# One step of a two-layer attention and RWKV-7 trunk: the mixer's state kept with keys as rows, and the samples' gate computed in the variance's bank

## The chip, the cores and the metric

The kernel runs as one launch on one core of a Trainium2 chip. The metric is device time in microseconds (us), the median of several runs. Five engines work side by side, each on its own queue of instructions: TensorE (PE in the profile; its weight loads have a row of their own, PEld), VectorE (DVE), ScalarE (ACT), GpSimd (POOL) and SyncE (SP), which here only issues DMAs.

## The reference

Two layers, 1024 prompt positions and 8 sample positions, width 1024, all in fp32. Each layer projects its input, runs windowed attention on one half of the columns and an RWKV-7 mixer with 8 heads of 64 on the other, projects both back, and adds a feed-forward part of width 4096. The change is in the mixer:

```
def step(S, inp):                                   # S: [value, key] for each head
    r_t, w_t, k_t, v_t, a_t, b_t = inp
    sa = einsum('bhvk,bhk->bhv', S, a_t)
    S = S * w_t[:, :, None, :] + sa[..., None] * b_t[:, :, None, :] + v_t[..., None] * k_t[:, :, None, :]
    return S, einsum('bhvk,bhk->bhv', S, r_t)
S_T, y = lax.scan(step, wkv0, xs)
mu = y.mean(-1); var = square(y - mu).mean(-1)      # per head
y = (y - mu) * rsqrt(var + GN_EPS) * gn_g + gn_b
y = (y + bonus) * g                                 # g = sigmoid(g_lo) @ gate_up
```

## The kernel before

**Work.** The prompt is cut into two halves of 512 positions; the 8 samples ride with the second. For each layer and half, the dense stream (`dense_stream`, `half`, `in_proj`) does the projections and the feed-forward part as matmuls in fp32r, three for each product (lines 389 to 391: high times high, low times high, high times low), with 256 to 512 moving columns. Beside it run the attention (`att_stream`), the mixer and the samples' attention (`kv_stream`).

**The mixer.** A unit is 256 positions of one pair of heads; there are 2 layers x 2 halves x 4 pairs x 2 = 32 units, each cut into four chunks of 64 positions (`cc` = 0 to 3, `tb, c = divmod(cc, 2)`). The first head of the pair lies on partitions 0 to 63, the second on 64 to 127. `stage1` prepares a unit, `stage2` carries the state through it, and `normed` does the GroupNorm and the gate. In `stage2`, after the inversion of the chunks' triangular matrices (lines 1308 to 1356), come two parts:

- The **pO part** (lines 1358 to 1376): for c = 0 and 1, a bank `o3` takes Pt times LB in its columns 0 to 127 and TV times LB in columns 128 to 255 (line 1370: lhsT is TV, 64 wide, and the contraction runs over all 128 partitions). One half of those 64 + 64 columns is the chunk's own share of the output y, the other its share of the new state. VectorE makes FG from columns 0 to 127.
- The **carry steps** (lines 1378 to 1395), one for each `cc`: the state Z, with keys as rows, is the stationary operand of line 1384, which adds to both halves of `o3`. The half that is the state then has values as rows and keys as columns. VectorE copies it to `St` (line 1386), TensorE transposes it with a product by the identity into the bank `pz` (line 1391), and VectorE scales it by the decay into the next Z (line 1393). The very first unit of a prompt starts without a state, so its first step has no product with Z.

**The gate.** `normed` sums y by a product with a block matrix (line 1417) and computes the gate for the 256 positions (line 1418) in one bank `pgm`, then the sum of squares (line 1431) in a bank `pgv`. In the last unit of a pair in the second half (8 units) a third bank, `pgd`, takes the gate of the 8 samples (line 1423); this stands ahead of the copy of the prompt's gate out of `pgm` (line 1426). All three have the tag "o", of which there are two banks; `o3` and line 1308's `pBV` use it as well. The tag "r" has one bank.

**The order on TensorE** is written at build time by the class `Streams` (lines 147 to 260): each stream is a generator that yields (planned cost, bank tag held and for how long, delay before its next piece, bank tag wanted). The planner always takes the first stream in the order s2 (stage2), norm, s1, att, post, kv that is ready, and otherwise the dense stream; delays are multiplied by 1.2 in the first phase and 2.2 later (`SLK`), and a turn away from the dense stream costs 280 planned ns. One turn can hold pieces of several streams. At run time TensorE executes that order strictly; the other engines' orders are made by the build's own scheduler.

Line 1004 is a gate of the dense stream: late in the first half's feed-forward part of the last layer it waits until the second half's mixer, attention and sample parts are all planned. In the attention, line 1623 delays a tile's transposition by 2500 + 4 x 640 planned ns for the widest tile, and line 1640 its output product.

Of the trace's names: `dps` are the dense banks, `pS`, `pET`, `pFT`, `po`, `pof` the attention's banks, `E` its scores, `pdo` those of `kv_stream`. A matmul in plain fp32 leaves two records in the trace (x4 is two matmuls); one in fp32r leaves one. "64*64" is the array tile that is used (rows * columns), "64x128" the output's partitions or rows and its columns.

Of the kernel before, what the change touches and what calls it, by code (L numbers as in the profile page):

```python
# [10 lines left out]
F32 = mybir.dt.float32  # L11
# [3 lines left out]
ALU = mybir.AluOpType  # L15
# [6 lines left out]
NB = 8  # L22
# [13 lines left out]
UN = 256  # L36
NU = HB // UN
# [229 lines left out]
def body(ctx, tc, I, O):  # L267
# [17 lines left out]
    def bank(tag, name):  # L285
        return ps.tile([128, 512], F32, tag=tag, bufs=BANKS[tag], name=name)
# [5 lines left out]
    def C(name):  # L292
        a, n = CAT[name]
        return cst[:, a:a + n]

    ident = C("ident")
    istk = C("istk")
# [805 lines left out]
    dd = {}  # L1103
# [207 lines left out]
    def stage2(l, h, p, u, s, st, Z, Zp):  # L1311

        AR, Wd, LB, TV, X, XT, bv, _ = st

        def other(c):
            return slice(64 * (1 - c), 64 * (1 - c) + 64)

        def halfof(t, c):
            return t.rearrange("p (b c) h s x -> p c h b s x", c=2)[64 * c:64 * c + 64, c]

        for lv in range(2):
            pb = bank("r", "pT1")
            q = small(pb, 0, lambda h, tb, i, c, r: (LB[r, h, 2 * tb + c, 128 * (1 - c):128 * (1 - c) + 64], X[r, i, :]))
            T1 = rq.tile([128, 4, 64], F32, tag="T1", name="T1")
            q0 = q
            if lv == 0:
                q = small(bank("o", "pBV"), 0, lambda h, tb, i, c, r: (
                    LB[other(c), h, 2 * tb + c, 128 * (1 - c):128 * (1 - c) + 64], TV[other(c), 2 * tb + c, h, 0, :]))
                q4 = q.rearrange("p (h b) t -> p h b t", h=2)
            A.copy(T1, q0)  # L1330
            if lv == 0:
                for c in range(2):
                    (A.copy if c else V.tensor_copy)(halfof(TV, c)[:, :, :, 1, :], q4[64 * c:64 * c + 64])
            yield (1050 if lv == 0 else 530, ("r", 900), 1500, "r")
            pb = bank("r", "pX")
            q = small(pb, 0, lambda h, tb, i, c, r: (T1[r, i, :], XT[r, i, :]))
            if lv == 0:
                q2 = small(pb, 256, lambda h, tb, i, c, r: (XT[r, i, :], T1[r, i, :]))
                V.copy_predicated(X, mk(0), q2)
            V.copy_predicated(XT, mk(2 * lv + 1), q)  # L1340
            yield (1050 if lv == 0 else 530, ("r", 900), 1500, "r")
        pb = bank("r", "pPQ")
        for tb in range(2):
            for hd in range(2):
                for c in range(2):
                    r = slice(64 * c, 64 * c + 64)
                    j = hd * 2 + tb
                    PE.matmul(pb[r, j * 128:j * 128 + 128], XT[r, j, :], TV[r, 2 * tb + c, hd, :, :], start=True, stop=True)  # L1348
        Pt = rq.tile([128, 4, 64], F32, tag="T1", name="Pt")
        q4 = pb.rearrange("p (h b s x) -> p h b s x", h=2, b=2, s=2)  # L1350
        V.tensor_copy(Pt.rearrange("p (h b) x -> p h b x", h=2), q4[:, :, :, 0, :])
        for c in range(2):
            A.copy(halfof(TV, c)[:, :, :, 0, :], q4[64 * c:64 * c + 64, :, :, 1, :])
        FG = rq.tile([128, 4, 128], F32, tag="FG", name="FG")
        Oc = []
        yield (970, ("r", 1000), 1300, "o")
        for c in range(2):
            pb = bank("o", f"pO{c}")
            o3 = pb.rearrange("p (b x) -> p b x", b=2)
            Oc.append(o3)  # L1360
            r = slice(64 * c, 64 * c + 64)
            for tb in range(2):
                for hd in range(2):
                    hs = slice(64 * hd, 64 * hd + 64)
                    PE.matmul(o3[hs, tb, 0:128], Pt[r, hd * 2 + tb, :], LB[r, hd, 2 * tb + c, 64 * c:64 * c + 128],  # L1365
                              start=(tb == 0), stop=True, skip_group_check=True)
            for tb in range(2):
                for hd in range(2):
                    hs = slice(64 * hd, 64 * hd + 64)
                    PE.matmul(o3[hs, tb, 128:256], TV[:, 2 * tb + c, hd, 0, :], LB[:, hd, 2 * tb + c, 64 * c:64 * c + 128],  # L1370
                              start=False, stop=True, skip_group_check=True)
            F4 = FG.rearrange("p (b c) x -> p c b x", c=2)[:, c]
            f0, g0 = 64 * (1 - c), 64 * c
            V.tensor_tensor(F4[:, :, f0:f0 + 64], AR[:, :, 320 * c:320 * c + 64], o3[:, :, f0:f0 + 64], op=ALU.subtract)
            V.tensor_tensor(F4[:, :, g0:g0 + 64], bc(istk, [(0, 2), (1, 64)]), o3[:, :, g0:g0 + 64], op=ALU.subtract)
            yield (960, None, 0 if c == 0 else 900, None if c == 0 else "r")
        note("lb", s)
        for cc in range(4):
            tb, c = divmod(cc, 2)
            o3 = Oc[c]  # L1380
            if Z is not None:
                for hd in range(2):
                    hs = slice(64 * hd, 64 * hd + 64)
                    PE.matmul(o3[hs, tb, 128:256], Z[hs, :], FG[hs, cc, :], start=False, stop=True, skip_group_check=True)
            St = rp.tile([128, 64], F32, tag="St", bufs=2, name="St")
            V.tensor_copy(St, o3[:, tb, 128 + 64 * c:192 + 64 * c])
            yield (280, None, 900, "r")
            pz = bank("r", "pz")
            for hd in range(2):
                hs = slice(64 * hd, 64 * hd + 64)  # L1390
                PE.matmul(pz[hs, 0:64], St[hs, :], istk[hs, :], start=True, stop=True)
            Z = Zp[:, p, :] if cc == 3 else rp.tile([128, 64], F32, tag="Z", bufs=2, name="Z")
            V.tensor_scalar(Z, pz[:, 0:64], Wd[:, cc, 64:65], None, op0=ALU.mult)
            if cc < 3:
                yield (130, ("r", 650), 900, None)
        y = rq.tile([128, 256], F32, tag="y", name="y")
        for c in range(2):
            A.copy(y.rearrange("p (b c t) -> p c b t", c=2, t=64)[:, c], Oc[c][:, :, 192 - 64 * c:256 - 64 * c])
        if h == 1 and u == NU - 1:
            yield (200, ("r", 650), 900, "r")  # L1400
            pz = bank("r", "pzf")
            for hd in range(2):
                hs = slice(64 * hd, 64 * hd + 64)
                PE.matmul(pz[hs, 0:64], Z[hs, :], istk[hs, :], start=True, stop=True)
            Zo = rp.tile([128, 64], F32, tag="Zo", name="Zo")
            V.tensor_copy(Zo, pz[:, 0:64])
            S.dma_start(O["wkv_p"][l, 0, 2 * p:2 * p + 2].rearrange("h v k -> (h v) k"), Zo)
        ys[s] = (y, bv)
        note("ch", s)
        yield (300, ("r", 700), 500, None)  # L1410

    def normed(l, h, p, u, s, gup, gs):

        y, bv = ys.pop(s)
        yield (0, None, 900, "o")
        pb = bank("o", "pgm")
        PE.matmul(pb[:, 0:256], C("blk"), y, start=True, stop=True)
        PE.matmul(pb[:, 256:512], gup, gs[:, 0:256], start=True, stop=True)
        V.scalar_tensor_tensor(y, pb[:, 0:256], -1.0 / 64, y, op0=ALU.mult, op1=ALU.add)
        if h == 1 and u == NU - 1:  # L1420
            yield (860, ("o", 1000), 0, "o")
            pz = bank("o", "pgd")
            PE.matmul(pz[:, 0:8], gup, gs[:, UN:UN + NB], start=True, stop=True)
            V.tensor_copy(dd["gsd"][:, p, :], pz[:, 0:8])
        gg = gs[:, 0:256]
        A.copy(gg, pb[:, 256:512])
        sq = rq.tile([128, 4, 128], F32, tag="FG", name="gq").rearrange("p a b -> p (a b)")[:, 0:256]
        A.activation(sq, y, AF.Square)
        yield (860, ("o", 1000), 1800, "o")
        pb = bank("o", "pgv")  # L1430
        PE.matmul(pb[:, 0:256], C("blk"), sq, start=True, stop=True)
        A.activation(sq, pb[:, 0:256], AF.Ln, bias=epsc[:, 1:2], scale=1.0 / 64)
        A.activation(sq, sq, AF.Exp, scale=-0.5)
        V.scalar_tensor_tensor(y, y, pv(l, "gng", p), sq, op0=ALU.mult, op1=ALU.mult)
        V.scalar_tensor_tensor(y, y, pv(l, "gnb", p), bv[:, 0:256], op0=ALU.add, op1=ALU.add)
        V.tensor_tensor(y, y, gg, op=ALU.mult)
        S.dma_start(d_rw[l][h][p, :, u * UN:u * UN + UN], y)
        yield (430, ("o", 2000), 0, None)
# [464 lines left out]
```

## Time and profile before

| | |
|---|---|
| runs before | 3280.85 us median of 3 (3280.17 to 3285.87) |
| profiled execution | 3282.56 us, span on the core 3280.7 us |
| PE busy | 3130.2 us, 95% |
| PEld busy | 2656.7 us, 81% |
| DVE busy | 2064.6 us, 63% |
| ACT busy | 1445.1 us, 44% |
| POOL busy | 983.3 us, 30% |
| HBM | 119 GB/s over the span |

The span runs from the first to the last instruction that the profiler recorded. A busy PE is one that has a matmul under way, also one that waits inside the array for its turn, so the busy share alone doesn't say how close to its peak it works: for that the distance between the starts of neighbouring matmuls has to be read in the timeline.

### The profile page before, as it was taken

The page shows a single profiled execution, that of the slowest core. Times are in us where ns is not written, and L with a number is a line of the kernel's source. Part 1 is how long each engine was busy: PE and PEld are TensorE (multiplying, and loading weights), DVE is VectorE, ACT ScalarE, POOL GpSimd, SP SyncE. Part 2 cuts the span into 40 slices and gives each one's busy share as a digit, 9 for nine tenths or more (in the row PEclk, how much of TensorE's full clock was granted, in tenths as well). Part 3 has the DMA queues.
Part 4 walks back from the last instruction along what each step waited for, and adds up shares of the span by engine and source line. Part 5 has one row for each costly group of instructions (what it writes and reads, how often), then busy time and mean ns, then how long its engine had stood idle before and what let it go on. Part 6 is the DMA issues. An engine that isn't in the chain of part 4 may idle for free. (4 is left out here: it accounts for less than half of the span.)

```text
span 3280.7 us, 65951 instructions
## 1 busy us (share of the span) xinstructions
PE 3130.2 (95%) x24732; PEld 2656.7 (81%) x24732; DVE 2064.6 (63%) x4703; ACT 1445.1 (44%) x3266; POOL 983.3 (30%) x1841
## 2 busy tenths in 40 slices
PE   9999999899999999999999999998999999899998
PEld 7768887777777787788999999877767777889997
DVE  5666667855557476677665576568655664875556
ACT  4445454544433364454443345444434333543334
POOL 1443335521221134463121122456121201620012
PEclk9999999999999999999999999999999999999999
DMA  7544445344343355533333236543343434423332
GB/s 230 153 136 128 129 136 164 85 124 126 111 114 103 98 157 164 157 102 105 89 96 90 89 96 185 152 133 100 97 119 106 119 107 125 135 82 91 94 89 83
DMA packets 370503, 393.58 MB, mean 120 GB/s; under 512 B 145816, under 2 KB 223080, under 8 KB 370184
## 3 DMA queue, kind: packets, MB, share of 16 engines
q10 hardware_dynamic: 121152, 213.44, 22.0%
q1 hardware_dynamic: 249032, 175.93, 18.9%
q8 instruction: 195, 3.19, 0.4%
q14 instruction: 124, 1.02, 0.1%
HBM read 325.30 MB, written 63.97 MB: 119 GB/s over the span
## 5 line engine op out<-in xcount | busy, mean ns | idle before, releaser
L389 PE MATMUL dps<-xh,wh 128*128 128x256 f32 (+3 forms) x2984 | 974.1, 326 | 14.9 <-ACT wh L362 6.5
L390 PE MATMUL dps<-xl,wh 128*128 128x256 f32 (+3 forms) x2984 | 947.7, 318 | 11.0 <-DVE xl L781 8.0
L391 PE MATMUL dps<-xh,wl 128*128 128x256 f32 (+3 forms) x2984 | 943.8, 316 | 1.7 <-DVE wl L363 1.6
L362 ACT CAST wh<-wr 128x512 fp32r<-128x512 f32 (+1 forms) x772 | 474.6, 616 | 818.2 <-PE dps L390 759.5
L363 DVE TENSOR_TENSOR wl<-wr,wh 128x512 fp32r<-128x512 f32 (+1 forms) x772 | 579.5, 751 | 357.1 <-ACT wh L362 335.9
L389 PEld LDWEIGHTS dps<-xh,wh 128*128 128x128 f32 x2984 | 567.6, 190 | 75.9 <-issue 18.1
L390 PEld LDWEIGHTS dps<-xl,wh 128*128 128x128 f32 x2984 | 567.7, 190 | 49.1 <-DVE xl L781 12.2
L391 PEld LDWEIGHTS dps<-xh,wl 128*128 128x128 f32 x2984 | 567.4, 190 | 40.5 <-DVE wl L363 3.9
L389 PE MATMUL dps<-hh,wh 128*128 128x512 f32 (+2 forms) x1600 | 527.5, 330 | 9.1 <-ACT lnm L731 3.9
L390 PE MATMUL dps<-hl,wh 128*128 128x512 f32 (+2 forms) x1600 | 513.5, 321 | 3.5 <-DVE mx L1615 1.5
L391 PE MATMUL dps<-hh,wl 128*128 128x512 f32 (+2 forms) x1600 | 512.8, 321 | 0.0
L389 PEld LDWEIGHTS dps<-hh,wh 128*128 128x128 f32 x1600 | 304.4, 190 | 42.5 <-issue 9.6
L390 PEld LDWEIGHTS dps<-hl,wh 128*128 128x128 f32 x1600 | 304.7, 190 | 24.9 <-DVE hl L852 2.8
L391 PEld LDWEIGHTS dps<-hh,wl 128*128 128x128 f32 x1600 | 304.3, 190 | 22.9
L1234 POOL TENSOR_TENSOR tm<-BL,XB 32x15 f32<-32x15 f32 (+7 forms) x480 | 146.7, 306 | 394.2 <-DMA BL<-d_el 348.6
L995 DVE TENSOR_TENSOR t<-dps,t 128x256 f32<-128x256 f32 (+1 forms) x240 | 123.7, 516 | 165.3 <-PE dps L391 164.6
L1236 POOL TENSOR_TENSOR XB<-XB,tm 32x15 f32<-32x15 f32 (+7 forms) x480 | 156.6, 326 | 34.6
L748 POOL TENSOR_TENSOR ln<-ln,lsq 128x256 f32<-128x256 f32 (+1 forms) x112 | 90.8, 811 | 247.4 <-ACT lsq L746 243.4
L963 DVE CAST hh<-rl 128x256 fp32r<-128x256 f32 (+2 forms) x200 | 73.8, 369 | 96.3 <-ACT rl L962 93.2
L737 POOL TENSOR_TENSOR t<-t,ln 128x256 f32<-128x256 f32 (+1 forms) x32 | 27.8, 904 | 350.3 <-ACT ln L731 350.3
L961 ACT ACTIVATE rl<-dps 128x256 f32<-128x256 f32 (+2 forms) x200 | 88.3, 442 | 97.1 <-PE dps L391 90.5
L389 PE MATMUL dps<-hh,xh 128*128 128x256 f32 (+1 forms) x368 | 110.0, 299 | 13.2 <-DVE t L1028 5.8
(345 smaller groups left out, 5080.4 us busy)
## 6 DMA issues: line engine op xcount, KB each, us to landing
wr<-in_w_ff_up ACTq DMA_DIRECT2D x272, 256.0 KB
wr<-in_w_ff_down ACTq DMA_DIRECT2D x256, 256.0 KB
wr<-in_w_in ACTq DMA_DIRECT2D x220, 256.0 KB
stg<-d_qkv SPq DMA_DIRECT2D x128, 128.0 KB
wr<-in_w_out ACTq DMA_DIRECT2D x64, 256.0 KB
z<-d_z SPq DMA_DIRECT2D x24, 384.0 KB
d_qkv<-qe SPq DMA_DIRECT2D x128, 64.0 KB
kvc<-in_cache_k SPq DMA_DIRECT2D x32, 256.0 KB
```

The source lines that it names most:

```text
L362: self.copies.append(A.copy(h[:, :, :m], w[:, :, :m]))
L363: V.tensor_tensor(lo[:, :, :m], w[:, :, :m], h.bitcast(F32)[:, :, :m], op=ALU.subtract)
L389: PE.matmul(p[:m, :n], wh[:, wk % 4, :m], hi, start=(i == 0), stop=False)
L390: PE.matmul(p[:m, :n], wh[:, wk % 4, :m], lo, start=False, stop=False)
L391: PE.matmul(p[:m, :n], wl[:, wk % 4, :m], hi, start=False, stop=(i == last))
L737: G.tensor_tensor(t, t, self.cm[:, c0:c0 + n], op=ALU.subtract)
L748: G.tensor_tensor(s2, s2, sq, op=ALU.add)
L961: A.activation(r, p[:, :n], AF.Relu)
L963: V.tensor_copy(hh[:, c0:c0 + n], r)
L995: V.tensor_tensor(to, p[:, :n], to, op=ALU.add)
L1234: G.tensor_tensor(tv, bc(BL[:, 17 * j + 1:17 * j + 2], [(1, m), (0, j + 1)]), bc(XB[:, 16 * j:16 * j + 1], [(0, m), (1, j + 1)]), op=ALU.mult)
L1236: G.tensor_tensor(xv, xv, tv, op=ALU.add)
```

## The change

In the pO part, the 128 columns of TV times LB are cut into two products of 64 columns. The one for y stays as it was; in the one for the state the operands change places, so that the state's share has keys as rows. In the carry steps the same is done with Z and FG: for the state's half FG is the stationary operand and Z the moving one. What stands in `o3` is then already [key, value], and the scaling by the decay reads it there: the copy `St`, the transposition `pz` and their turn in the plan are gone. The yields change with it (a step was 280 and 130 planned ns in two turns, each with a delay of 900; it is now one of 280 with a delay of 1000). In `normed`, the samples' gate leaves its own bank and turn, and is computed in columns 256 to 263 of `pgv`, ahead of the sum of squares.

```diff
@@ stage2, pO part
+            f0, g0 = 64 * (1 - c), 64 * c
             for tb in range(2):
                 for hd in range(2):
                     hs = slice(64 * hd, 64 * hd + 64)
-                    PE.matmul(o3[hs, tb, 128:256], TV[:, 2 * tb + c, hd, 0, :], LB[:, hd, 2 * tb + c, 64 * c:64 * c + 128],
+                    PE.matmul(o3[hs, tb, 128 + f0:192 + f0], TV[:, 2 * tb + c, hd, 0, :], LB[:, hd, 2 * tb + c, 64:128],
+                              start=False, stop=True, skip_group_check=True)
+                for hd in range(2):
+                    hs = slice(64 * hd, 64 * hd + 64)
+                    PE.matmul(o3[hs, tb, 128 + g0:192 + g0], LB[:, hd, 2 * tb + c, 2 * g0:2 * g0 + 64], TV[:, 2 * tb + c, hd, 0, :],
                               start=False, stop=True, skip_group_check=True)
...
-            yield (960, None, 0 if c == 0 else 900, None if c == 0 else "r")
+            yield (960, None, 0 if c == 0 else 900, None)
@@ stage2, carry steps
-            o3 = Oc[c]
+            o3, f0, g0 = Oc[c], 64 * (1 - c), 64 * c
             if Z is not None:
                 for hd in range(2):
                     hs = slice(64 * hd, 64 * hd + 64)
-                    PE.matmul(o3[hs, tb, 128:256], Z[hs, :], FG[hs, cc, :], start=False, stop=True, skip_group_check=True)
-            St = rp.tile([128, 64], F32, tag="St", bufs=2, name="St")
-            V.tensor_copy(St, o3[:, tb, 128 + 64 * c:192 + 64 * c])
-            yield (280, None, 900, "r")
-            pz = bank("r", "pz")
-            for hd in range(2):
-                hs = slice(64 * hd, 64 * hd + 64)
-                PE.matmul(pz[hs, 0:64], St[hs, :], istk[hs, :], start=True, stop=True)
+                    PE.matmul(o3[hs, tb, 128 + g0:192 + g0], FG[hs, cc, g0:g0 + 64], Z[hs, :], start=False, stop=True,
+                              skip_group_check=True)
+                for hd in range(2):
+                    hs = slice(64 * hd, 64 * hd + 64)
+                    PE.matmul(o3[hs, tb, 128 + f0:192 + f0], Z[hs, :], FG[hs, cc, f0:f0 + 64], start=False, stop=True,
+                              skip_group_check=True)
             Z = Zp[:, p, :] if cc == 3 else rp.tile([128, 64], F32, tag="Z", bufs=2, name="Z")
-            V.tensor_scalar(Z, pz[:, 0:64], Wd[:, cc, 64:65], None, op0=ALU.mult)
+            V.tensor_scalar(Z, o3[:, tb, 128 + g0:192 + g0], Wd[:, cc, 64:65], None, op0=ALU.mult)
             if cc < 3:
-                yield (130, ("r", 650), 900, None)
+                yield (280, None, 1000, None)
@@ normed
-        if h == 1 and u == NU - 1:
-            yield (860, ("o", 1000), 0, "o")
-            pz = bank("o", "pgd")
-            PE.matmul(pz[:, 0:8], gup, gs[:, UN:UN + NB], start=True, stop=True)
-            V.tensor_copy(dd["gsd"][:, p, :], pz[:, 0:8])
...
         pb = bank("o", "pgv")
+        if h == 1 and u == NU - 1:
+            PE.matmul(pb[:, 256:256 + NB], gup, gs[:, UN:UN + NB], start=True, stop=True)
+            V.tensor_copy(dd["gsd"][:, p, :], pb[:, 256:256 + NB])
         PE.matmul(pb[:, 0:256], C("blk"), sq, start=True, stop=True)
```

The line numbers of the new kernel are 1371 and 1375 (pO part), 1388 and 1392 (the two products of a carry step), 1395 (the scaling) and 1429 (the samples' gate).

The planner lays out the whole of TensorE's order anew. Three places show what moves.

TensorE in the first unit, two carry steps, before (1384 is the product with Z, 1391 the transposition; 1607 and 1608 are attention scores, 1132 and 1137 the next unit's `stage1`):

```order
L1384 MATMUL pO_1330<-FG,Z 64x128 x2
L1607 MATMUL pS<-kS,qS 128x384
L1608 MATMUL pS<-kS,qL 128x384
L1132 MATMUL psg<-dup,lo_1419 128x128 x2
L1137 MATMUL psg<-lo_1419,iup 128x256
L1391 MATMUL pz<-cst,St 64x64 x2
L389 MATMUL dps<-xh_89,wh 128x512
```

and the same place now:

```order
L1388 MATMUL pO_1319<-Z,FG 64x64 x2
L1392 MATMUL pO_1319<-FG,Z 64x64 x2
L1607 MATMUL pS<-kS,qS 128x384
L1608 MATMUL pS<-kS,qL 128x384
L1132 MATMUL psg<-dup,lo_1428 128x128 x2
L1137 MATMUL psg<-lo_1428,iup 128x256
L1388 MATMUL pO_1334<-Z,FG 64x64 x2
L1392 MATMUL pO_1334<-FG,Z 64x64 x2
L389 MATMUL dps<-xh_89,wh 128x512
```

Where one step's transposition stood, the next step's products stand now: a step takes one turn in place of two.

TensorE at the end of a pair of the second half in layer 0, before (1404 is the final state's transposition, 1417 and 1418 fill `pgm`, 1308 belongs to the next unit):

```order
L1404 MATMUL pzf<-cst,Zp 64x64 x2
L1162 MATMUL pn<-sq,cst 128x264
L1170 MATMUL pcs<-cst,sg 128x128 x2
L1417 MATMUL pgm<-y,cst 128x256
L1418 MATMUL pgm<-gs,gup 128x256
L1308 MATMUL pT_8353<-X,LB 64x64 x8
L1308 MATMUL pBV<-TV,LB 64x64 x8
L1423 MATMUL pgd<-gs,gup 128x8
L1630 MATMUL pET<-cst,E 128x128 x2
```

and such a place now:

```order
L1419 MATMUL pgm<-y,cst 128x256
L1420 MATMUL pgm<-gs,gup 128x256
L1162 MATMUL pn<-sq,cst 128x264
L1170 MATMUL pcs<-cst,sg 128x128 x2
L389 MATMUL dps<-xh_88,wh 128x256
L390 MATMUL dps<-xl_90,wh 128x256
L391 MATMUL dps<-xh_88,wl 128x256
L389 MATMUL dps<-xh_89,wh 128x256
L390 MATMUL dps<-xl_91,wh 128x256
L391 MATMUL dps<-xh_89,wl 128x256
L1429 MATMUL pgv<-gs,gup 128x8
L1431 MATMUL pgv<-gq,cst 128x256
```

The samples' gate has moved from between two groups of the next unit to just ahead of the variance's product.

TensorE at the gate of line 1004 in layer 1, before (1818 and 1824 end `kv_stream`, 730 is the first work behind the gate):

```order
L389 MATMUL dps<-hh,wh 128x512
L390 MATMUL dps<-hl,wh 128x512
L391 MATMUL dps<-hh,wl 128x512
L1818 MATMUL pdo<-kvc,dsc 32x128 x8
L1824 MATMUL pdo_33174<-cst,dms 128x128
L730 MATMUL lnc<-t,onec 128x256 x2
L389 MATMUL dps<-xh_88,wh 128x512
```

and now, where the last attention tile's transpositions (1630, 1644) and output products (1653, 1662) stand there too, behind five dense triples since its scores:

```order
L389 MATMUL dps<-hh,wh 128x512
L390 MATMUL dps<-hl,wh 128x512
L391 MATMUL dps<-hh,wl 128x512
L1824 MATMUL pdo_32982<-cst,dms 128x128
L1630 MATMUL pET<-cst,E 128x128 x8
L1644 MATMUL pFT<-cst,E 128x128 x2
L1653 MATMUL po<-ET,vT 64x128 x8
L1662 MATMUL pof<-FT,vT 64x64 x8
L730 MATMUL lnc<-t,onec 128x256 x2
L389 MATMUL dps<-xh_88,wh 128x512
```

The attention's last tile has come to stand at the gate, with no dense work between its own pieces.

Counted over the whole order, the carry steps and the pO part have 256 + 256 + 480 matmuls where they had 256 + 240 + 256 (the products Pt times LB stay), and the dense matmuls are the same 14,904. Changes of the array's tile or of the dtype (fp32r or fp32) from one matmul to the next go from 1633 to 1456. Of these, turns from fp32r into an fp32 group on a part of the array go from 464 to 380, turns from such a group back to fp32r from 337 to 294, and all turns out of such a group (to another shape or to fp32r) from 937 to 789.

## Rows read from the trace of the kernel before

**Rows 1.** The page's first part: busy time, share of the span, instructions.

```profile
span 3280.7 us, 65951 instructions
PE 3130.2 (95%) x24732; PEld 2656.7 (81%) x24732; DVE 2064.6 (63%) x4703; ACT 1445.1 (44%) x3266; POOL 983.3 (30%) x1841
```

**Rows 2.** Two stretches: width, busy of PE, PEld, DVE, ACT, POOL, clock, DMA.

```profile
2000.00:2720.00 720.00, 683.85 (x5351) 544.46 (x5351) 448.87 (x1063) 304.72 (x707) 222.97 (x441) 0.98 0.42 121
2720.00:3281.00 561.00, 525.49 (x4002) 504.19 (x3991) 345.85 (x647) 224.04 (x458) 117.69 (x129) 0.98 0.33 99
```

**Rows 3.** PE's waits: who waited for whom; total us, times, longest.

```profile
PE pgd L1423 <- ACT gs L1426: 11.3, 6, 4.1
...
PE pz L1391 <- DVE St L1386: 8.2, 3, 6.7
...
PE pO L1384 <- DVE Z L1393: 5.5, 7, 1.0
...
PE pgv L1431 <- ACT gq L1428: 1.4, 1, 1.4
```

**Rows 4.** Timeline of PE in the first unit's carry steps: start, duration, instruction.

```profile
124.66 0.39 PE L390 MATMUL dps<-xl,wh 128*128 128x512 f32 x1
124.89 0.40 PE L391 MATMUL dps<-xh,wl 128*128 128x512 f32 x1
125.22 0.33 PE L1391 MATMUL pz<-cst,St 64*64 64x64 f32 x4
125.48 0.66 PE L1653 MATMUL po<-ET,vT 128*64 128x128 f32 x8
...
128.71 0.44 PE L1384 MATMUL pO<-FG,Z 64*64 64x128 f32 x4
129.08 0.44 PE L1607 MATMUL pS<-kS,qS 128*128 128x384 f32 x1
...
130.96 0.50 PE L389 MATMUL dps<-xh,wh 128*128 128x512 f32 x1
131.29 0.39 PE L390 MATMUL dps<-xl,wh 128*128 128x512 f32 x1
```

**Rows 5.** Timeline of PE, the pO part's second product of c = 1.

```profile
119.00 0.66 PE L1370 MATMUL pO<-LB,TV 128*64 128x128 f32 x8
119.59 0.66 PE L1630 MATMUL pET<-cst,E 128*128 128x128 f32 x4
```

**Rows 6.** Timeline of PE, an attention product on 128 rows with 64 columns.

```profile
2709.70 0.69 PE L1662 MATMUL pof<-FT,vT 128*64 128x64 f32 x16
2710.31 0.70 PE L1417 MATMUL pgm<-y,cst 128*128 128x256 f32 x2
```

**Rows 7.** Groups by line: records | busy us, mean ns | idle before, releaser.

```profile
L1370 PE MATMUL pO<-LB,TV 128*64 128x128 f32 x512 | 42.5, 288 | 0.4 <-ACT TV L1353 0.4
...
L1384 PE MATMUL pO<-FG,Z 64*64 64x128 f32 x384 | 41.8, 295 | 5.5 <-DVE Z L1393 5.5
...
L1386 DVE COPY St<-pO 128x64 f32<-128x64 f32 x128 | 28.2, 220 | 46.8 <-PE pO L1384 46.1
...
L1384 PE MATMUL pO<-FG,Zp 64*64 64x128 f32 x96 | 10.5, 295 | 0.0
```

**Rows 8.** Timeline around the longest wait for `St`, on DVE and on PE.

```profile
227.54 3.40 DVE L535 TENSOR_TENSOR xl<-t,xh 128x520 fp32r<-128x520 f32 x2 [4.89 <-ACT xh L534]
...
231.19 0.48 PE L1391 MATMUL pz<-cst,St 64*64 64x64 f32 x4 [6.71 <-DVE St L1386]
```

**Rows 9.** Timeline of the attention's last tile, on PE, DVE and ACT.

```profile
2681.30 0.39 PE L1608 MATMUL pS<-kS,qL 128*128 128x512 f32 x1
...
2684.34 0.55 DVE L1619 TENSOR_SCALAR E<-E,mx 128x640 f32<-128x640 f32 x1
...
2694.73 1.09 PE L1630 MATMUL pET<-cst,E 128*128 128x128 f32 x8
...
2696.44 0.58 ACT L1635 COPY ET<-pET 128x512 f32<-128x512 f32 x1
```

More of the change, by code (lines that the diff above doesn't have):

```diff
@@ L1369, in stage2 @@
                     hs = slice(64 * hd, 64 * hd + 64)
-                    PE.matmul(o3[hs, tb, 128:256], TV[:, 2 * tb + c, hd, 0, :], LB[:, hd, 2 * tb + c, 64 * c:64 * c + 128],
+                    PE.matmul(o3[hs, tb, 128 + f0:192 + f0], TV[:, 2 * tb + c, hd, 0, :], LB[:, hd, 2 * tb + c, 64:128],
[3 more added lines that the diff above has]
+                    PE.matmul(o3[hs, tb, 128 + g0:192 + g0], LB[:, hd, 2 * tb + c, 2 * g0:2 * g0 + 64], TV[:, 2 * tb + c, hd, 0, :],
                               start=False, stop=True, skip_group_check=True)
             F4 = FG.rearrange("p (b c) x -> p c b x", c=2)[:, c]
-            f0, g0 = 64 * (1 - c), 64 * c
             V.tensor_tensor(F4[:, :, f0:f0 + 64], AR[:, :, 320 * c:320 * c + 64], o3[:, :, f0:f0 + 64], op=ALU.subtract)
             V.tensor_tensor(F4[:, :, g0:g0 + 64], bc(istk, [(0, 2), (1, 64)]), o3[:, :, g0:g0 + 64], op=ALU.subtract)
-            yield (960, None, 0 if c == 0 else 900, None if c == 0 else "r")
+            yield (960, None, 0 if c == 0 else 900, None)
         note("lb", s)
```

## The prediction

> **What bounds the kernel now.** I read the busy times first. TensorE has a matmul under way for 3130.2 us of a span of 3280.7, 95%, and no other engine passes 63% [rows 1]. The stretches of time say the same of each part: while the mixer of the last half runs, PE is busy 683.85 us of 720, and behind it 525.49 of 561 [rows 2]. So the bound is TensorE, in two kinds of time: what its instructions take in the array (some 3130 us), and the 150 us in which it has nothing. The list of waits then tells who holds it up: no single wait is large, the first on the list is 11.3 us in all [rows 3]. Removing work from VectorE is therefore worth nothing by itself; what counts is how long TensorE's own instructions take and how often it stands still. For the former I read the timeline, and there the distance from one start to the next, since the durations overlap.
>
> The timeline shows two things. First, a small fp32 product pays for more than its columns. The transposition of two heads (four records) starts at 125.22 and the next group at 125.48, 0.26 us; the product with Z (four records of 128 columns) takes from 128.71 to 129.08, 0.37 us [rows 4]. Second, turning to such a group costs extra on both sides: dense matmuls of 512 columns start 0.23 us apart, the last one ahead of the transposition has 0.33 us, and the first one behind a group also 0.33 (130.96 to 131.29) [rows 4]. That is 0.10 us going in and 0.10 coming back, besides the group itself.
>
> **The change, part by part.**
>
> *Carry steps.* There are 128 of them, as the copies `St` count [rows 7], and 384 + 96 records of line 1384, four to a step, make 120 with a product [rows 7]. Before, such a step took 0.37 + 0.26 = 0.63 us in two turns [rows 4]. Now it is eight records of 64 columns in one turn. For their price I take the attention's product of the same 64 columns: sixteen records in 0.61 us (2709.70 to 2710.31) [rows 6]. Against four records in 0.26, twelve more cost 0.35, or 0.029 each; eight records then take 0.26 + 4 x 0.029 = 0.38. That saves 0.25 us x 120 = 30 us. The 8 steps without a product lose their transposition, 8 x 0.26 = 2 us. Together **32 us**. If a record of 64 columns took as long as one of 128, which is (0.59 - 0.37) / 4 = 0.055 us [rows 4, 5], the step would be 0.37 + 4 x 0.055 = 0.59 and the saving 0.04 x 120 + 2 = 7 us: that is the other end. I take the first, because rows 6 are the same shape and dtype.
>
> *pO part.* Eight records of 128 columns on all 128 rows (0.59 us, 119.00 to 119.59 [rows 5]) become sixteen of 64 columns on all 128 rows. Rows 6 are exactly that form: 0.61 us. There are 512 / 8 = 64 such parts [rows 7], so this costs 64 x 0.02 = **1.3 us**; the other end, at 0.055 us for each of the eight added records, is 64 x 0.44 = 28 us.
>
> [...]
>
> *Turns.* The order has 84 turns fewer from dense work into a small group (464 to 380) and 43 fewer straight back (337 to 294). At 0.10 us each [rows 4] that is 8.4 + 4.3. Of the 148 turns out of a small group that are gone, 128 are the transpositions' own, whose cost lies in their 0.26; the other 20 at 0.10 are 2.0. Together **14.7 us**. The number is the planner's doing: a step that needs one turn shares it less often with dense work on both sides. If the price were 0.05 it would be 7.
>
> So TensorE's own time falls by 32 - 1.3 + 14.7 = **45 us**.
>
> *The samples' gate.* Its two records and its copy of 8 columns stay and move with it, ahead of the variance's product; they cost what they did. What goes is its wait: 11.3 us in six of the eight places, each time for the copy of `pgm`'s gate on ACT [rows 3], which the code puts behind it. In its new place it stands behind that copy anyway. The variance's product waited only 1.4 us in all its 32 places [rows 3]. But in the last units VectorE was late as well, and part of that lateness will meet `pgv` instead. I take **8 us** between 0 and 11.3.
>
> *The copy `St`.* Line 1391 waited 8.2 us for it, in three places [rows 3]. One is 6.71 us, and there VectorE was stuck for 4.89 us on the load of the second half's input (line 535, waiting for ACT) [rows 8]. Whatever needs VectorE next will wait there instead, so I count only the rest, **1.5 us**, between 0 and 8.2. Nobody else on TensorE waits for these 128 copies (28.2 us of VectorE [rows 7]), so the freed VectorE time counts nothing.
>
> *The gate at line 1004.* The mixer's chain gets shorter by a turn per step, so its last unit ends earlier than the attention. Now the attention's last tile stands at the gate without cover. From its last scores to the end of its softmax it took 3.6 us (2681.30 to 2684.34 + 0.55), and from the first transposition to the end of the copy of ET 2.3 us (2694.73 to 2696.44 + 0.58) [rows 9]. The new order has five dense triples (15 x 0.23 = 3.5 us) after the scores, which cover the first, and about 1.1 us of transpositions inside the second. I put **2 us** of new waiting there. From below it is nothing. From above: the planner itself allows 2.2 x 5.06 and 2.2 x 1.72 us and 3 us for the load, 18 us in all.
>
> *No cost:* the final state's eight transpositions stay, no DMA is added or removed, and SP's and POOL's queues get nothing new.
>
> Sum: 45 + 8 + 1.5 - 2 = 53 us. The profiled execution took 3282.56 us, its span 3280.7 and 1.9 around it; so it would take 3229.6. The median of the runs is 1.7 us lower, 3280.85, so the forecast is 3280.85 - 53 = **3228 us**, 1.6% faster.
>
> **The rivals.**
>
> *The waits come back.* The whole order is laid out anew, and what no longer stands still in one place may do so in another. With the array's 45 us alone the time is 3236; with the gate's 18 us besides, 3254. For it: VectorE's lateness is behind most waits and doesn't change. Against: the two largest removed waits had their cause in the removed instructions' place.
>
> *Small products bound by their weight loads.* If 64 columns cost what 128 do (the other ends above), the steps give 7 us, the pO part takes 28, the turns give 15, the waits 7.5: a gain of 1.5 us, 3279, no change. [...] Rows 6 speak against it.
>
> *Z comes late (slower).* A step now consists of products, one scaling on VectorE, and the next products, and in the first order piece only four lines of work stand between two steps. If VectorE is busy with a long instruction at that point, all of TensorE waits, dense work included. To be slower by over 0.2% (about 6.6 us, what a measurement of this kernel can tell from no change) it would have to eat 53 + 6.6 us, 0.5 us at each of 120 steps; at 0.6 us the time would be 3300. Before, both hand-offs of a step, 248 in all, cost 5.5 + 8.2 us [rows 3], 0.055 us each. Ten times that is hard to reach with one hand-off fewer.
>
> *More than forecast.* All of the removed waits stay away and the shorter chain takes some ten others along: 45 + 11 + 8 + 10 = 74, 3206.
>
> **How the numbers follow.** I give the forecast 0.67, the waits that come back 0.20, more than forecast 0.06, the weight loads 0.04, a late Z 0.03. The first three are faster: 0.93; the fourth is no change: 0.04; the last slower: 0.03. The range goes from 3206, where the most favourable ends meet, to 3254, where the array's saving is all that is left and the gate takes its most. The weight loads and the late Z lie outside it, and what else I haven't seen.
>
> **What would show it.** Right: eight records of lines 1388 and 1392 within about 0.38 us, the sixteen of 1371 and 1375 within about 0.6, PE's busy time down by some 40 us, no wait of line 1429 over a few us, a short wait of `pET`, `po` at the end of the last mixer. Wrong: runs of 64-column records at 0.055 us each (weight loads), waits of line 1388 for Z (line 1395) that sum to tens of us (late Z), or PE's idle time above 150 us while its busy time falls (the waits come back).

## The result and the profile after

The changed kernel takes **3244.88 us** (median of 4 runs, 3242.63 to 3245.86); the kernel before took 3280.51 us on the same chip (4 runs, 3278.67 to 3285.87). The ratio is 0.9888 with a 95% interval of 0.9871 to 0.9905: some 36 us or 1.1% faster. The forecast was 3228, so 17 us of the 53 didn't come, and the time lies where the rival of the waits that come back had put it (3236 to 3254). It is also inside the forecast's range (3206 to 3254), whose upper end is that rival's.

The page's first part of the kernel after:

```profile
span 3244.0 us, 66793 instructions
PE 3089.7 (95%) x25212; PEld 2662.6 (82%) x25212; DVE 2041.2 (63%) x4575; ACT 1442.2 (44%) x3266; POOL 974.9 (30%) x1841
```

Beside [rows 1], PE is busy 40.5 us less, the span is 36.7 us shorter, and so PE's idle time has grown from 150.5 to 154.3 us. The two stretches of [rows 2] of the kernel after (width, busy time of PE, PEld, DVE, ACT, POOL, granted clock, DMA share, GB/s):

```profile
2000.00:2720.00 720.00, 684.23 (x5444) 550.33 (x5444) 440.89 (x1013) 302.90 (x694) 237.46 (x451) 0.97 0.42 121
2720.00:3244.00 524.00, 490.39 (x3826) 475.82 (x3824) 329.13 (x620) 210.70 (x436) 102.21 (x113) 0.98 0.32 97
```

The share of PE is what it was. In the mixer's stretch 720 us hold 5444 matmul records instead of 5351 with the same busy time, at a granted clock of 0.97 instead of 0.98; part of the added records are the cut products, so the count alone shows no gain.

The timeline of PE shows what the new products take. It gives start, duration, instruction, and in brackets the idle time ahead of it with what ended it; first the second products of a pO part, then a carry step:

```profile
118.62 0.34 PE L1371 MATMUL pO<-LB,TV 128*64 128x64 f32 x4
118.78 0.29 PE L1375 MATMUL pO<-TV,LB 128*64 128x64 f32 x4
118.90 0.29 PE L1371 MATMUL pO<-LB,TV 128*64 128x64 f32 x4
119.02 0.29 PE L1375 MATMUL pO<-TV,LB 128*64 128x64 f32 x4
119.23 0.65 PE L1365 MATMUL pO<-LB,Pt 64*64 64x128 f32 x8
...
126.06 0.33 PE L1388 MATMUL pO<-Z,FG 64*64 64x64 f32 x4
126.22 0.28 PE L1392 MATMUL pO<-FG,Z 64*64 64x64 f32 x4
126.44 0.66 PE L1653 MATMUL po<-ET,vT 128*64 128x128 f32 x8
```

The sixteen records of the pO part take 0.61 us (118.62 to 119.23), the eight of a carry step 0.38 (126.06 to 126.44). Both are the forecast's figures, and they hold elsewhere: wherever such a group stands at full clock and without a wait, its mean distance to the next group is 0.38 us for a carry step (117 places) and 0.61 for a pO part (59 places). The waits of PE are where it went otherwise (who waited for whom; total us, times, longest):

```profile
PE pn L1170 <- ACT sg L569: 13.2, 7, 4.4
PE pgm L1419 <- ACT y L1400: 12.8, 6, 4.5
PE pgv L1431 <- DVE gsd L1430: 11.3, 6, 6.2
...
PE pO L1388 <- DVE Z L1395: 3.7, 5, 1.5
...
PE po L1653 <- ACT ET L1635: 1.2, 2, 0.8
```

The wait for the samples' gate has the same size as the one that was removed (11.3 us in six places [rows 3]), only that its releaser is now VectorE's copy `gsd`. Two others stand out: `pn` for `sg` (2.6 us, 2 places before), and `pgm` for `y`, which did not occur. Of the smaller ones, `pde` for `dsc` (6.1 us, one place) is new, and `pdw` for `sg` is 7.6 us where it was 3.3; no experiment is about these. The wait for `St` (8.2 us [rows 3]) is gone.

**Where the time went.** In some stretches the records show a granted clock of 0.5, the lower of the two levels in the traces of before and after (0.5 and 1.00). Each of the 29 in the kernel after begins during a wait of PE or at most 2.2 us behind the end of one. One of the long ones:

```profile
582.00:586.00 4.00, 4.00 (x23) 3.80 (x22) 4.00 (x3) 2.23 (x5) 3.93 (x7) 0.60 0.37 126
586.00:594.00 8.00, 8.00 (x102) 7.32 (x102) 7.71 (x20) 2.80 (x9) 2.82 (x5) 1.00 0.35 100
```

These two windows of the kernel after stand behind a wait of 6.17 us that ended at 581.33: 23 matmul records in 4 us at 0.60, then 102 in 8 us at 1.00. So PE's busy time has to be split. In stretches at 0.5 I count half of the busy time as lost; busy time less that is an estimate of what the array's work would take at full clock (1.00). Half is at the upper end: the starts of dense matmuls of 512 columns are mostly 0.43 us apart at 0.5 and 0.23 at 1.00, those of 256 columns 0.21 and 0.12, which makes 43 to 47% in the kernel after; at 45% the array's work would fall by 49 us where the table has 50. It repeats well: two executions of one kernel agree to 2.3 us in it, in the three kernels of the new mixer that were profiled twice, where their busy times differ by up to 9.6. By the trace of each profiled execution (us):

| kernel | span | idle | lost at clock 0.5 | work at full clock |
|---|---|---|---|---|
| before | 3280.7 | 150.5 | 47.3 | 3082.9 |
| after | 3244.0 | 154.3 | 57.0 | 3032.7 |
| difference | -36.7 | +3.8 | +9.7 | -50.2 |

The array's work has fallen by 50 us; 13.5 of them are given back, in idle time and at the lower clock.

### The profile page after: what moved, and what is told of

Same layout as the page of the kernel before. It is cut to its first block, busy times and chain, and to the rows that moved or that the text cites. A ratio compares the mean times of both kernels' runs of the same rounds, so it can differ in the third digit from the quotient of the medians.

```text
span 3244.0 us, 66793 instructions
## 1 busy us (share of the span) xinstructions
PE 3089.7 (95%) x25212; PEld 2662.6 (82%) x25212; DVE 2041.2 (63%) x4575; ACT 1442.2 (44%) x3266; POOL 974.9 (30%) x1841
## 4 chain that ended last, share of the span: by engine, by line
PE 73%; DVE 10%; DMA 7%; POOL 4%; issue 3%; ACT 3%; SPq 1%; ACTq 0%; DVEq 0%; POOLq 0%
PE dps L389 19%; PE dps L390 18%; PE dps L391 18%; DVE t L778 2%; PE pX L1308 1%; DVE wl L363 1%; PE po L1653 1%; DMA z<-d_z 1%; PE pET L1630 1%; PE pS L1607 1%; PE pS L1596 1%; DMA stg<-d_qkv 1%; POOL XB L1236 1%; PE pO L1365 1%; PE pT L1308 1%
## 5 line engine op out<-in xcount | busy, mean ns | idle before, releaser
L1234 POOL TENSOR_TENSOR tm<-BL,XB 32x15 f32<-32x15 f32 (+7 forms) x480 | 150.5, 314 | 370.9 <-DMA BL<-d_el 262.2
L737 POOL TENSOR_TENSOR t<-t,lnm 128x256 f32<-128x256 f32 (+1 forms) x80 | 69.2, 897 | 216.6 <-ACT lnm L731 212.7
```

The source lines that it names most:

```text
L737: G.tensor_tensor(t, t, self.cm[:, c0:c0 + n], op=ALU.subtract)
L1234: G.tensor_tensor(tv, bc(BL[:, 17 * j + 1:17 * j + 2], [(1, m), (0, j + 1)]), bc(XB[:, 16 * j:16 * j + 1], [(0, m), (1, j + 1)]), op=ALU.mult)
```

## The experiments

All ratios are to the kernel before on the same chip, with 95% intervals. There were four questions: whether the copy `gsd` holds up the variance's product, whether the state's change alone gives the gain, what the added weight loads cost, and whether the two larger waits can be removed by their distance in the plan.

**1. The copy of the samples' gate behind the variance's product.** In the changed kernel, one line moves:

```diff
         if h == 1 and u == NU - 1:
             PE.matmul(pb[:, 256:256 + NB], gup, gs[:, UN:UN + NB], start=True, stop=True)
-            V.tensor_copy(dd["gsd"][:, p, :], pb[:, 256:256 + NB])
         PE.matmul(pb[:, 0:256], C("blk"), sq, start=True, stop=True)
+        if h == 1 and u == NU - 1:
+            V.tensor_copy(dd["gsd"][:, p, :], pb[:, 256:256 + NB])
```

> The changed kernel with one line moved: the samples' copy out of pgv is written behind the variance's product, not ahead of it, so that the product no longer waits for that copy. TensorE's order is the same. Theory A (the six waits of the variance's product for the copy, 11.3 us, replaced the six waits of pgd, also 11.3, and each long wait is followed by a stretch at half the clock): these waits fall to the 3.6 us for gq or a little over, and the time to 3233 +- 5. Rival (the copy only stood last in line, and the product then waits for gq on ACT, which is as late): 3243 to 3247.

Measured: ratio 0.9852 [0.9830, 0.9875], 48 us below before and so where the expectation had it. The waits of PE:

```profile
PE pn L1170 <- ACT sg L569: 15.3, 7, 4.4
PE pgm L1419 <- ACT y L1400: 10.0, 5, 4.4
...
PE pgv L1430 <- ACT gq L1425: 5.0, 2, 3.8
```

The wait for `gsd` is gone. A smaller one of the variance's product for its own operand `gq` stands there (3.6 us in two places in the changed kernel). TensorE's order is the same as in the changed kernel, and so are the two products; so the wait came from the copy's place. (VectorE's order, which the build makes, differs at 95 of 4575 places, so not all of the time need be that wait's.) Why an eight-column copy costs so much is seen in the changed kernel's timeline around one of the six places, first on PE, then on VectorE:

```profile
581.33 1.19 PE L1431 MATMUL pgv<-gq,cst 128*128 128x256 f32 x2 [6.17 <-DVE gsd L1430]
582.32 1.06 PE L1630 MATMUL pET<-cst,E 128*128 128x128 f32 x4
```

```profile
576.78 2.00 DVE L363 TENSOR_TENSOR xl<-wr,xh 128x512 fp32r<-128x512 f32 x2
578.71 0.94 DVE L1191 TENSOR_TENSOR AR<-z,Wd 128x256 f32<-128x256 f32 x1
579.57 0.94 DVE L1190 TENSOR_TENSOR BK<-f,Wi 128x256 f32<-128x256 f32 x1
580.44 0.68 DVE L922 SCALAR_TENSOR_TENSOR t<-xo,dps 128x512 f32<-128x512 f32 x1
581.03 0.15 DVE L1430 COPY gsd<-pgv 128x8 f32<-128x8 f32 x1
```

The copy itself takes 0.15 us. But it stands behind VectorE's whole queue, of which the last five instructions are shown, and the product behind it in the program writes other columns of the bank that it reads. PE therefore waits for the whole queue, 6.17 us here.

**2. Each part alone.** First the mixer's change alone: the changed kernel, with `normed` as it was before (the samples' gate in its own bank `pgd`):

```diff
+        if h == 1 and u == NU - 1:
+            yield (860, ("o", 1000), 0, "o")
+            pz = bank("o", "pgd")
...
         pb = bank("o", "pgv")
-        if h == 1 and u == NU - 1:
-            PE.matmul(pb[:, 256:256 + NB], gup, gs[:, UN:UN + NB], start=True, stop=True)
-            V.tensor_copy(dd["gsd"][:, p, :], pb[:, 256:256 + NB])
```

> Only the mixer's part of the change: the gate of the samples keeps its own bank pgd and its own turn, as before. Theory A: PE's busy time falls by about 40 us as in the changed kernel, the waits of pgd stay (some 8 to 11 us), the waits of pgm for y are as in the changed kernel; 3245 +- 8. Rival (the gate's move alone brought part of the gain): 3255 or more.

Measured: 0.9850 [0.9831, 0.9869], as in experiment 1 on the same chip. The changed kernel's 0.9888 [0.9871, 0.9905] is from another comparison, but the intervals do not overlap. The mixer's part alone gives all of the gain; that the gate's part, as it is written, takes some of it away is likely, and no run shows it side by side. Neither `pgd` nor `gsd` is among PE's waits here, against the expectation, by which the waits of `pgd` would stay: in the new order the wait of 11.3 us goes without the gate's move. `pn` for `sg` has 16.1 us and `pgm` for `y` 11.0.

Then the gate's part alone, in the kernel before: the change's hunk in `normed` and nothing else.

> Only the gate's part: the samples' gate joins pgv, the mixer is as before. Theory A: one wait goes, an equal one comes (the variance's product for the copy): 3280 +- 6, no measurable gain. The prediction's own step (8 us, with the shorter half clock besides): 3265 to 3273.

Measured: 0.9986 [0.9973, 0.9999], at the edge of what can be told from no change. The wait is of the same kind as in the changed kernel:

```profile
PE pgv L1429 <- DVE gsd L1428: 9.9, 8, 3.7
```

And the same with the copy behind the product, as in experiment 1:

> The gate's part alone on the mixer of before, with the samples' copy behind the variance's product. Theory A: the 9.9 us of waits for the copy go, and with them 8 to 14 us of the time of before (3267 to 3273 where before is 3280.5). Rival (that wait only covers another one): within 4 us of before.

Measured: 0.9969 [0.9957, 0.9982], about 10 us below before, with no wait for `gsd` and 1.1 us of the variance's product for `gq`. So the term that the prediction had for this part exists with the mixer of before (8 us forecast), if the copy stands behind the product. With the new mixer it does not show: with the gate moved in this way (experiment 1) and without its move the ratio is the same, 0.9852 and 0.9850, on one chip.

**3. The weight loads.** The kernel before, with the products of lines 1370 and 1384 cut into two of 64 columns each, stationary operands and turns as they were:

```diff
-                    PE.matmul(o3[hs, tb, 128:256], Z[hs, :], FG[hs, cc, :], start=False, stop=True, skip_group_check=True)
+                    PE.matmul(o3[hs, tb, 128 + 64 * x:192 + 64 * x], Z[hs, :], FG[hs, cc, 64 * x:64 * x + 64],
+                              start=False, stop=True, skip_group_check=True)
```

> The kernel before, with the products of lines 1370 and 1384 cut into two of 64 columns each, operands not exchanged, St and pz as before; same yields, so the same turns. Theory A (a record of 64 columns costs half): 64 x 0.02 + 120 x 0.01 = 2.5 us more, 3279 to 3287. Rival (weight loads bind, 0.055 us for each added record): 512 + 480 added records, 54 us more, 3330.

Measured: 1.0056 [1.0036, 1.0075], some 18 us slower, which neither expectation had. The timeline on PE, a pO part and a carry step:

```profile
118.53 0.69 PE L1371 MATMUL pO<-LB,TV 128*64 128x64 f32 x16
119.14 0.66 PE L1365 MATMUL pO<-LB,Pt 64*64 64x128 f32 x8
...
129.46 0.45 PE L1387 MATMUL pO<-FG,Z 64*64 64x64 f32 x8
129.84 0.44 PE L1611 MATMUL pS<-kS,qS 128*128 128x384 f32 x1
```

Sixteen records take 0.61 us and eight take 0.38, and the work at full clock is 3085.8 us, 2.9 more than before. So the added loads cost what the forecast's theory says (64 x 0.02 + 120 x 0.01 = 2.5 us). The trace puts it in its place: counted from each record's start to the next one's, less the idle time, at full clock, the cut products take 3.0 us more and no other group changes by more than 0.5. The other 20 us of the profiled span (3303.8) are 7.2 us more idle time and 13.0 more lost at clock 0.5. In the waits many entries are a little longer or shorter; the one that grows most is `pdw` for `sg`, 8.7 us where it was 3.3. The cut changes no turn of TensorE's plan, and the traces show PE's groups in the same order. VectorE's order differs at 279 of 4703 places and ScalarE's at 136 of 3266; that this is behind the 20 us is the nearest reading, but no run shows it.

**4. More distance for `y`.** On top of experiment 1, `normed` waits a further 1500 planned ns (which `after` does not multiply by 2.2, as the expectation has it) behind the end of a unit's carry steps:

```diff
-                        yield after("ch", s)
+                        yield after("ch", s, lat=1500)
```

> e1 (the samples' copy behind the variance's product), and the norm stream starts a unit 1500 planned ns (times 2.2) later after its state is through. Theory B (with the transposition's turn gone, y's mean stands one turn nearer to the copy of y, and meets VectorE's queue): the waits of pgm for y fall from 10.0 us to under 3, and the time by 6 to 12 us against e1, the half clock behind them included. Rival (y is late because VectorE is behind by more than a turn): the waits stay above 7 us, and the time stays within 4 us of e1.

Measured: 0.9821 [0.9803, 0.9839]. No wait of `pgm` for `y` is left. The head of PE's list and the page's first part:

```profile
PE pn L1170 <- ACT sg L569: 13.8, 10, 3.1
PE dps L389 <- DVE t L1028: 11.8, 12, 1.8
PE dps L390 <- DVE xl L781: 10.6, 12, 1.9
```

```profile
span 3220.1 us, 66744 instructions
PE 3074.9 (95%) x25212; PEld 2648.8 (82%) x25212; DVE 2028.4 (63%) x4575; ACT 1443.4 (45%) x3266; POOL 978.2 (30%) x1841
```

To compare it with experiment 1 on one chip, both ran again beside each other.

> e1 (only the samples' copy moved behind the variance's product) on the same chip as the next, so that the delay for y is told apart from the chip. Theories A and B: 0.984 to 0.989 of the kernel before, slower than e2 by some 10 us.

> e2 (e1 and the delay of 1500 for y) once more beside e1. Theory B: below e1 by 6 to 14 us, 0.980 to 0.984 of the kernel before, with the time at half the clock again some 35 us shorter than in the changed kernel. Rival (the first result of e2 was a matter of the chip): within 4 us of e1.

Measured: 0.9844 [0.9822, 0.9867] without the distance and 0.9817 [0.9798, 0.9836] with it. The medians differ by 6.2 us in the direction expected, at the low end of what was; the intervals still overlap, so this step alone is not proven. In the profiled executions the stretches at 0.5 sum to 116 us with the distance and 150 without. The runs without it spread from 3225.1 to 3243.6 us, those with it from 3221.7 to 3231.5; why is open.

The same line in the kernel before tells whether it is a gain of any order:

> The kernel before with the delay of 1500 for y alone. Theory B (there the transposition's turn already gave y its distance, and pgm waited for nothing): no gain, 3280 +- 8. Rival (the delay helps by itself, whatever the mixer): 8 us or more below the kernel before.

Measured: 0.9982 [0.9962, 1.0002]: no gain that can be told from none, where `pgm` had no wait to remove. But the medians lie 8.1 us apart here, more than the 6.2 above, so how much time the delay brings beyond what any other order brings stays open; that it removes the wait is shown.

**5. More distance for `sg`.** On top of experiment 1, the delay of `stage1` ahead of `pn` is doubled:

```diff
-            yield (400, ("a", 700), 2000, "a")
+            yield (400, ("a", 700), 4000, "a")
...
-            yield (860, ("a", 1100), 2000, "a")
+            yield (860, ("a", 1100), 4000, "a")
```

> e1, and stage1's turn behind the sigmoids gets a delay of 4000 planned ns in place of 2000. Theory C (before, the unit two places back held stage1 up longer than the delay did; now that unit is through earlier, and the sums pn and pcs stand close behind ACT's sigmoid): the waits of pn for sg fall from 15.3 us to under 5, the time by 8 to 15 us against e1. Rival (the waits follow ACT's load, not the distance): they stay above 10 us.

Measured: 0.9890 [0.9873, 0.9907]. On the same chip the changed kernel had 0.9919 [0.9901, 0.9937] (experiment 6), so the time is 6.6 us below it by the medians, with intervals that overlap, and not the 8 to 15 us below experiment 1 that were expected: that one has 0.9852 and 0.9844 in two other comparisons. The wait is off the list and others took its place:

```profile
PE dps L389 <- DVE t L952: 9.0, 3, 4.9
...
PE pS L1597 <- DVE mx L1604: 5.4, 1, 5.4
...
PE pET L1631 <- ACT sq L1179: 4.3, 1, 4.3
PE pS L1608 <- DVE ao L1656: 4.3, 4, 1.7
```

With both delays together:

> e1 with both delays. Theories B and C together: pgm for y under 3 us, pn for sg under 5, PE's idle time 125 to 132 us, the time 14 to 25 us below e1 (near 3215 where the kernel before takes 3280.5). Rival (waits only move to other places): idle stays at 140 us or more and the time within 6 us of e1.

Measured: 0.9894 [0.9877, 0.9911]. New at the head of the list:

```profile
PE pT L1308 <- DVE XT L1340: 13.1, 6, 4.7
...
PE pO L1388 <- DVE Z L1395: 9.9, 6, 3.3
```

Now products of the inversion (line 1308) and of the carry steps wait for VectorE, and the idle time is 152.9 us, where 125 to 132 were expected and experiment 1 has 143.3 and 147.5 in its two executions. The delays moved waits and took no idle time away, as the rival had it; the time is above the rival's too, which had it within 6 us of experiment 1.

**6. The changed kernel once more**, beside the runs of 4 and 5:

> The changed kernel once more, on the same chip as the three that follow, so that they can be compared with it directly. Every theory: 0.987 to 0.991 of the kernel before.

Measured: 0.9919 [0.9901, 0.9937] (3252.7 us beside 3281.09), just outside what was expected: a gain of 28 us by the medians where the first comparison had 36. Differences of this size between two comparisons have to be allowed for wherever ratios of two chips stand side by side. The fastest version is that of experiment 4: 0.9821 and 0.9817 in two comparisons, some 59 us below before, and in the first of them, on the chip of these runs, 29 us below the changed kernel.

## Why the forecast fell short

**The array's work: right, term by term.** The terms "carry steps" (0.25 us x 120, and 2), "pO part" (1.3) and "turns" (14.7) gave 45 us; the work at full clock fell by 50. It lies between 3032 and 3037 in all nine profiled executions with the new mixer, and between 3081 and 3087 in the five with the old one, whatever else was changed. The traces of before and after tell the terms apart, if each record is counted from its start to the next one's, less the idle time, at full clock. The carry steps with their transpositions take 31.8 us less (32 forecast), the second products of the pO part 1.2 more (1.3), and the dense matmuls, whose number is the same and which pay for turns at both ends, 15.7 less (14.7; 13.8 in the second profiled execution of the changed kernel). The 3.9 us that are left are spread over small groups: `pgd`, which is gone (1.8), and several of 1 to 2 us either way. The price of a step was read from products on another part of the array (128*64 in [rows 6], 64*64 in the steps), and it held. The other end (records of 64 columns at the price of 128) is refuted by experiment 3 and by the new rows: in the pO part the added records cost 1.2 us, not the 28 of that end.

**The samples' gate: wrong.** The step of the prediction that failed is "In its new place it stands behind that copy anyway". It weighed the old copy of `pgm` alone. It did not ask what the moved copy of 8 columns does in its new bank, where it stands ahead of a product. Its sign for being right, no wait of line 1429, came true and missed the wait, which is at the product behind that line (1431). Forecast -8, measured 0 against the old wait: 11.3 us in six places before and after. Experiment 1, and the last run of experiment 2, show that the copy's place is what decides over the wait. The mixer's part alone (experiment 2) shows besides that the old wait hung on the order: it went without any move of the gate.

**The waits that come back: the rival was right.** The prediction gave it a chance of 0.20, on the ground that the two largest removed waits had their cause in the removed instructions' place. What it left out is what the removed instructions had covered. The sign that it had named, idle time above 150 us, came true with 154.3, though the kernel before had 150.5 already. The groups by line show it, records | busy us, mean ns | idle time before and its releaser; in the kernel before

```profile
L1417 PE MATMUL pgm<-y,cst 128*128 128x256 f32 x64 | 20.7, 405 | 0.0
...
L1398 ACT COPY y<-pO 128x128 f32<-128x128 f32 x64 | 17.0, 266 | 36.6 <-DVE St L1386 36.5
```

and after

```profile
L1419 PE MATMUL pgm<-y,cst 128*128 128x256 f32 x64 | 21.7, 423 | 12.8 <-ACT y L1400 12.8
...
L1400 ACT COPY y<-pO 128x128 f32<-128x128 f32 x64 | 16.8, 262 | 39.4 <-DVE Zp L1395 27.5 <-DVE Z L1395 9.2 <-DMA wr<-in_w_in 2.3
```

ScalarE's copy of y out of the pO banks waited for VectorE's reading of the state out of them before (36.5 us for `St`), and it does now (27.5 and 9.2 for `Zp` and `Z`). Before, the transposition's turn and its delay lay between that reading and `pgm`, and PE waited for nothing. Without that turn the copy comes as late, and PE is there earlier. Counted from the end of a unit's last carry product over the 32 units, the copies of y are done after 0.6 to 6.3 us before and 0.6 to 6.4 after, while PE has come to `pgm` after 3.4 us at the least and 7.0 in the median before, and after 1.5 and 4.1 now. The added delay of experiment 4 makes that 3.2 and 6.7 again, and the wait is gone. One of the six places, on PE, ACT and VectorE of the kernel after:

```profile
1322.67 1.22 PE L1419 MATMUL pgm<-y,cst 128*128 128x256 f32 x2 [4.55 <-ACT y L1400]
```

```profile
1322.36 0.27 ACT L1400 COPY y<-pO 128x128 f32<-128x128 f32 x1 [2.21 <-DVE Zp L1395]
```

```profile
1317.15 1.82 DVE L818 TENSOR_TENSOR hl<-rw,hh 128x520 fp32r<-128x520 f32 x1 [0.61 <-ACT hh L817]
1318.89 0.68 DVE L363 TENSOR_TENSOR wl<-wr,wh 128x512 fp32r<-128x512 f32 x1
1319.58 2.37 DVE L684 TENSOR_TENSOR rm<-qe,tab 64x512 f32<-64x512 f32 x2
...
1322.06 0.26 DVE L1395 TENSOR_SCALAR Zp<-pO,Wd 128x64 f32<-128x64 f32 x1
```

VectorE is held by the making of two low parts (`hl`, `wl`) and then by two products of the position rotation (line 684) for 2.37 us; `Zp` comes behind them, `y` behind `Zp`, `pgm` behind `y`.

In the trace both PE's wait behind `gsd` and ScalarE's behind `Zp` and `Z` have one form: an engine waits for another engine's access to the same bank, though the columns or the values are not those that it needs. It is 11.3 us of PE for a read ahead of a write to other columns, and 36.7 us (27.5 and 9.2) of ScalarE for a read ahead of a read. The first goes when the copy is moved (experiment 1); no run moves the second, and what puts these waits there is not shown.

**`pn` for `sg`: not settled.** 13.2 us where it was 2.6. It comes with the new mixer (16.1 in experiment 2 without the gate's part; 5.4 with the gate's part alone), and a longer delay removes it without a gain.

**The copy `St`: right in the main.** Its wait of 8.2 us is gone; the forecast counted 1.5 of it, because what needs VectorE next would wait instead. That is what came: between 200 and 260 us, where its longest place was, PE waited for VectorE 7.9 us before and waits 5.5 after. VectorE stands still for ScalarE there as it did (5.42 us to 218.41), and the product `psg` waits 2.99 us for the `mx` behind that. **The gate at line 1004:** forecast +2 us, measured 1.1: there `pET` waits 0.62 us (at 2687.65, for VectorE's copy `dms` of the samples' part) and `po` 0.46 (at 2688.95). **Z late:** 3.7 us in five places, beside 5.5 before [rows 3], as the prediction argued.

**No term for the clock.** The sum had no line for what PE does behind a wait. The lost time at clock 0.5 is 9.7 us larger in the profiled execution after. How much of that belongs to the change is not settled: two executions of one kernel differ nearly as much (52.7 and 61.1 in experiment 1, 38.2 and 47.2 in experiment 4).

The balance: the array gave 50 us where 45 were forecast; the waits should have given 7.5 net, and idle time and clock took 13.5 instead. That makes the 36.7 us between the two profiled executions. Without the waits for `gsd` and `y` (experiment 4) the gain is 57 to 61 us by the medians, the forecast and a little more. That the time fell into the rival's stretch of 3236 to 3254 is in part luck: the upper end of that stretch was made with 18 us at the gate of line 1004, which took 1.1, and the array gave 5 us more than the stretch allowed for.

## What to carry to other kernels

Before removing an instruction, ask what its turn had covered: here the turn of a transposition of 0.26 us had kept six later groups from waiting 12.8 us in all. A small result that joins another's bank should be read behind the last write to that bank, not between two, since the reader's whole queue then stands between two matmuls: here 11.3 us of waits in six places, and none with the copy behind the product (experiment 1). And where an order is laid out anew, check a gain of one per cent against a change that should be neutral before it is put down to one of its parts: here a cut that added 3 us of work and left TensorE's order as it was made the kernel 18 us slower.

## What was not expected of the hardware

- A wait can cost PE more than its length. Behind the wait of 4.55 us that ended at 1322.67 the two records of `pgm`'s first product start 1.02 us ahead of the next product (1322.67 to 1323.69); the same two records in the kernel before took 0.43 (2394.57 to 2395.00). The lower clock level goes with it: the 5.4 us from 1322.6 on have a mean granted clock of 0.69, the next 8 us 1.00.
- The cut of experiment 3 added 992 records (25,724 on PE in place of 24,732): 2.9 us of work at full clock, 0.003 us a record, and yet some 18 us in the kernel's time.
